# A two-layer hybrid decoder trunk on one core: element-wise work of the attention stages moved from VectorE to GpSimd, and the modulation columns from GpSimd to VectorE

## The chip, the core and the metric

The kernel runs on one core of a Trainium2 chip. A core has five engines with a queue each, and each works through its queue in order: TensorE (in the profile PE; its weight loads are shown apart as PEld), VectorE (DVE), ScalarE (ACT), GpSimd (POOL) and SyncE (SP, which issues nearly all transfers here). They wait for one another through semaphores. Matmul results lie in PSUM, everything else on the core in SBUF; GpSimd works on SBUF alone. The metric is the device time of one execution in microseconds, the median of several runs.

## The reference

Two layers over 512 tokens of width 1024. In each, six vectors (shift, scale and gate, twice) are made from a condition c; then come attention with three kinds of heads and a gated MLP.

```
for layer in range(DEPTH):                      # 2
    mod = silu(c) @ w_mod[layer] + b_mod[layer]             # 6 x 1024
    shift1, scale1, gate1, shift2, scale2, gate2 = split(mod, 6)
    h = rmsnorm(x, g_attn) * (1 + scale1) + shift1
    proj = h @ w_in
    # A: 4 heads, rotary, difference of two softmaxes (weight lam), sub-norm
    # B: 6 heads, rotary, mixture of three dilated windows
    # C: 6 heads, softmax with a cumulative forget bias
    o = concat(A, B, C)
    x = x + gate1 * (o @ w_out)
    h = rmsnorm(x, g_mlp) * (1 + scale2) + shift2
    up = h @ w_up;  u, g = up[:D_FF], up[D_FF:]             # D_FF = 2816
    x = x + gate2 * ((silu(causal_conv3(g)) * u) @ w_down)
return rmsnorm(x, g_final)
```

The rotation of A and B (`apply_rope`) is `x1*cos - x2*sin, x2*cos + x1*sin`; the kernel orders the columns so that it becomes `q*cos + swapped(q)*sin`, where the swap exchanges neighbouring rows.

## The kernel before

Activations are kept transposed: features on the 128 partitions, the 512 tokens along the free axis. Each product of a weight and an activation is made of three matmuls (`mm3`, L265 to L267): both operands are split into a rounded high part and the rest, the low part, and high x high, low x high and high x low are added up in PSUM. The high part is a copy on ScalarE into a rounding type, the low part a subtraction (`source - high`).

*Weights.* `plan` lists all weights in the order of use, tiles of 128 x 1024 for the most part. The class `Weights` loads a tile into one of three `raww` buffers (`dma`, L148, from SP's queue), makes its high part on ScalarE (`hi`, L174) and its low part on VectorE (`lo`, L186), into two buffers each (`whi`, `wlo`). `pump`, called at the steps of the chunk in progress, runs this ahead: the load two weights ahead, high and low part one ahead. A chunk (`feat_q`) is 8 steps of 3 matmuls.

*The attention of a layer* works through eight pairs of heads in the order B0 B1 A0 C0 A1 C1 B2 C2. Each pair has 8 blocks (2 heads, 4 blocks of 128 queries): scores on TensorE (`emit_S`, L631 to L641, tile `s`), masked maximum on VectorE (`emit_max`, L654, tile `e`), exponential on ScalarE (L667), transposes on TensorE (L695, tile `pt`), high and low part of the weights' transpose (L714 ScalarE, L719 VectorE), and the product with the values (L741, L742, tile `po`). In between, `fill` puts in the projections for the next pair: one chunk of queries and one of keys (`qk_chunk`, PSUM tile `qkps`) and half of a value chunk (`v_half`, `vps`), and behind the last pair the output projection (`ops`).

*A chunk's result* is worked up by `qk_post`. For A and B: ScalarE copies `qkps` to `qf` (L469); two transfers write its rows, exchanged, to `sw` (L471, L472); VectorE multiplies `qf` by the cosines (L475) and `sw` by the sines (L477) and adds them (L479). For B (and C, which has no rotation) `stack_gen` then makes high and low parts of both heads' halves, 64 rows each (L436 ScalarE, L433 VectorE), and copies them so that one matmul takes high and low rows together (L447, L449). For A, `split_gen` makes one high and one low part (L254, L256), which transfers lay out in `res`. A pair's output gets its high and low part (`oh`, `ol`) from `split_gen` too.

*Modulation.* One column of `mod` (128 features) is the sum over 1024 products of a row of `w_mod` and silu(c) (`scb`, copied to all partitions). The first 16 columns are made at the start (tile `mu`). The other 32 of layer 0 and the 48 of layer 1 are made by `mod_stream` beside other work: 24 of them (16 to 39 of layer 0) during layer 0's attention, 56 during layer 0's MLP. Each column is loaded in two halves of 256 KB into three buffers (`rawm`, L240). In the attention stage a half goes through three engines: product on GpSimd (L221), sum by an accumulating copy on ScalarE (L224), addition on VectorE (L226). In the MLP one VectorE instruction does all (L228, a product with a running sum). A last small operation makes `1 + scale` times the norm's weight (L234).

*The order.* The code is written as generators that are stepped by `tick`; a scheduler then sorts each engine's instructions by its own estimate of when they can run. So a change of engine also moves instructions that it doesn't touch.

Of the kernel before, what the change touches and what calls it, by code (L numbers as in the profile page):

```python
# [30 lines left out]
def kernel(  # L31
# [34 lines left out]
    mrp = ctx.enter_context(tc.tile_pool(name="mrp", bufs=3))  # L66
# [43 lines left out]
    lp = const.tile([128, DEPTH, 4, 32], F32, name="lp")  # L110
# [27 lines left out]
    class Weights:  # L138
# [39 lines left out]
        def lo(self, upto):  # L178
            while self.nl < min(upto, len(plan)):
# [4 lines left out]
                raw = self.raw.pop(i)  # L184
                for c, m, h, lo in self.w[i]:
                    V.tensor_tensor(out=lo[:, 0:m], in0=raw[:, c:c + m], in1=h[:, 0:m].bitcast(F32), op=ALU.subtract)  # L186
# [24 lines left out]
    def mod_col(l, ci, raws, pool=False):  # L211
        part, m = divmod(ci, 8)
        prev = bm[:, l, ci:ci + 1]
        for half in range(2):
            raw = raws(half)
            yield
            dst = modc[:, l, ci:ci + 1]
            if half == 0:
                dst = sm.tile([128, 1], F32, tag="mp", name="mp")
            if pool:  # L220
                G.tensor_tensor(out=raw, in0=raw, in1=scb[:, 512 * half:512 * half + 512], op=ALU.mult)  # L221
                yield
                d2 = sm.tile([128, 1], F32, tag="mp", name="mq")
                A.activation(out=raw, in_=raw, func=AF.Copy, accum_out=d2)  # L224
                yield
                V.tensor_tensor(out=dst, in0=d2, in1=prev, op=ALU.add)  # L226
            else:
                V.tensor_tensor_reduce(out=raw, in0=raw, in1=scb[:, 512 * half:512 * half + 512], scale=1.0, scalar=prev,  # L228
                                       op0=ALU.mult, op1=ALU.add, accum_out=dst)
            prev = dst  # L230
            yield
        if part in (1, 4):
            g = gA if part == 1 else gM
            V.scalar_tensor_tensor(out=scl[:, l, part // 4, m:m + 1], in0=modc[:, l, ci:ci + 1], scalar=1.0,  # L234
                                   in1=g[:, l, m:m + 1], op0=ALU.add, op1=ALU.mult)

    def mod_stream(l, ci):
        def raws(half):
            raw = mrp.tile([128, 512], F32, tag="raw", name="rawm")
            nc.sync.dma_start(out=raw, in_=wmod[l, ci, :, 512 * half:512 * half + 512])  # L240
            return raw
        return mod_col(l, ci, raws, l == 0 and 16 <= ci < 40)
# [10 lines left out]
    def split_gen(src, hi, lo):  # L253
        A.activation(out=hi, in_=src, func=AF.Copy)  # L254
        yield
        V.tensor_tensor(out=lo, in0=src, in1=hi.bitcast(F32), op=ALU.subtract)  # L256
# [122 lines left out]
    def layer_attn(l, ap, mods, st, rt0):  # L379
# [49 lines left out]
        def stack_gen(src, side, res, pair=None):  # L429
            R = (H0, H1)  # L430

            def sub(out, h):
                V.tensor_tensor(out=out, in0=src[R[h]], in1=res[h][R[h]].bitcast(F32), op=ALU.subtract)  # L433
# [25 lines left out]
        def qk_post(idx, side, ps, kind):  # L459
# [13 lines left out]
            for _ in range(5):  # L473
                yield
            V.tensor_tensor(out=qf, in0=qf, in1=tb[:, 0, :], op=ALU.mult)  # L475
            yield
            V.tensor_tensor(out=sw, in0=sw, in1=tb[:, 1, :], op=ALU.mult)  # L477
            yield
            V.tensor_tensor(out=qf, in0=qf, in1=sw, op=ALU.add)  # L479
# [710 lines left out]
```

## Time and profile before

| | us |
|---|---|
| median of 3 runs | 1338.51 (1336.86 to 1346.54) |
| profiled execution, its own time | 1337.11 |
| its span, first to last instruction | 1335.3 |
| layer 0: first chunk matmul of the attention (`qkps` with `whi`) | at 64.1 |
| layer 0: first matmul of the MLP (`pg`) | at 315.5 |
| layer 1: first value matmul (`vps`) | at 689.4 |
| layer 1: first matmul of the MLP (`pg`) | at 953.4 |

The granted TensorE clock is 0.989 of full speed over the span. A row of the profile's groups gives line, engine, operation, output <- inputs, shapes, how often, then busy us and mean ns of one, and at the end how long the engine stood idle just before and what ended that. A row of a timeline starts with its start and its length in us; x2 means that neighbouring instructions of one kind are merged. Lengths of matmuls are modelled: a 128x512 matmul is shown with 0.39 us, but the next one starts 0.23 us after it, as they overlap.

### The profile page before, as it was taken

Reading aid. Unit: us, or ns where it says so; the run is one execution under the profiler, and the core shown is the slowest. Engines: PE = TensorE matmul, PEld = TensorE weight load, DVE = VectorE, ACT = ScalarE, POOL = GpSimd, SP = SyncE. Lnnn points to the kernel's source line nnn. Section 1 sums busy time; section 2 is a strip of 40 time slices with the busy share of each in tenths; the row PEclk is TensorE's granted clock in tenths of the full one; section 3 lists DMA queues with packets and bytes.
Section 4 is the critical chain, followed back from the end, with each engine's and each line's share of the span. In section 5 each row is a group of like instructions: output and inputs, shape, how many; then the busy total and the mean of one; then the engine's idle time right before and its main releaser. Section 6 shows DMA issues by size and latency. Waiting matters only on the chain.

```text
span 1335.3 us, 18235 instructions
## 1 busy us (share of the span) xinstructions
PE 1278.1 (96%) x6568; PEld 1058.2 (79%) x6568; DVE 868.8 (65%) x1733; ACT 671.5 (50%) x1254; POOL 94.1 (7%) x64
## 2 busy tenths in 40 slices
PE   4899999999999999999999999999999999999997
PEld 1688787778888878888898888878878888888886
DVE  6888989868888886433347787875754444443232
ACT  5577888954433333322336677785543333333231
POOL 5232423400000000000000000000000000000000
PEclk8899999999999999999999999999999999999999
DMA  9445553432777775333333234212133333332331
GB/s 373 146 136 158 165 156 129 137 113 82 249 251 256 247 253 152 91 97 93 113 113 94 85 108 128 78 57 89 49 108 95 97 94 96 95 91 87 103 99 63
DMA packets 68127, 174.44 MB, mean 131 GB/s; under 512 B 9410, under 2 KB 11730, under 8 KB 68036
## 3 DMA queue, kind: packets, MB, share of 16 engines
q1 hardware_dynamic: 66884, 172.16, 40.9%
q8 instruction: 52, 0.85, 0.3%
q10 hardware_dynamic: 1088, 1.05, 0.2%
q14 instruction: 39, 0.32, 0.1%
q0 software_dynamic: 64, 0.06, 0.0%
HBM read 159.41 MB, written 2.10 MB: 121 GB/s over the span
## 4 chain that ended last, share of the span: by engine, by line
PE 59%; DVE 9%; DMA 6%; ACT 4%; issue 2%; SPq 0%; DVEq 0%; ACTq 0%
PE dps L265 6%; PE dps L267 6%; PE dps L266 6%; DMA rawm<-in_wmod_dram 5%; PE pg L266 4%; PE pu L265 4%; PE pg L267 4%; PE pu L267 4%; PE pu L266 4%; PE pg L265 4%; DVE wlo L186 2%; PE ops L265 2%; PE ops L266 2%; PE ops L267 2%; DVE rawm L228 2%
## 5 line engine op out<-in xcount | busy, mean ns | idle before, releaser
L186 DVE TENSOR_TENSOR wlo<-raww,whi 128x1024 fp32r<-128x1024 f32 (+3 forms) x188 | 228.2, 1214 | 232.0 <-ACT whi L174 227.8
L174 ACT ACTIVATE whi<-raww 128x1024 fp32r<-128x1024 f32 (+3 forms) x188 | 194.5, 1035 | 335.8 <-PE dps L266 137.8
L266 PE MATMUL pg<-hl,whi 128*128 128x512 f32 (+1 forms) x368 | 143.1, 389 | 0.5 <-DVE hl L314 0.2
L265 PE MATMUL pg<-hh,whi 128*128 128x512 f32 (+1 forms) x368 | 141.5, 385 | 1.6 <-ACT whi L174 1.6
L265 PE MATMUL pu<-hh,whi 128*128 128x512 f32 (+1 forms) x368 | 142.3, 387 | 0.0
L267 PE MATMUL pg<-hh,wlo 128*128 128x512 f32 (+1 forms) x368 | 141.0, 383 | 1.1 <-DVE wlo L186 1.1
L267 PE MATMUL pu<-hh,wlo 128*128 128x512 f32 (+1 forms) x368 | 140.6, 382 | 0.1
L266 PE MATMUL pu<-hl,whi 128*128 128x512 f32 (+1 forms) x368 | 140.7, 382 | 0.0
L265 PE MATMUL dps<-mh,whi 128*128 128x512 f32 x308 | 121.5, 394 | 0.0
L267 PE MATMUL dps<-mh,wlo 128*128 128x512 f32 x308 | 121.5, 394 | 0.0
L266 PE MATMUL dps<-ml,whi 128*128 128x512 f32 x308 | 121.2, 393 | 0.0
L667 ACT ACTIVATE e<-e,nm 128x256 f32<-128x256 f32 (+3 forms) x160 | 88.9, 556 | 33.9 <-DVE nm L654 30.6
L265 PE MATMUL qkps<-hh,whi 128*128 128x512 f32 x224 | 95.7, 427 | 1.0 <-ACT qf L469 0.7
L907 ACT ACTIVATE y<-y 128x512 f32<-128x512 f32 x44 | 27.8, 632 | 127.0 <-DVE y L904 117.0
L266 PE MATMUL qkps<-hl,whi 128*128 128x512 f32 x224 | 89.5, 400 | 0.0
L267 PE MATMUL qkps<-hh,wlo 128*128 128x512 f32 x224 | 89.4, 399 | 0.0
L654 DVE CUSTOM_DVE_ANT_0 e<-s,cst 128x256 f32<-128x256 f32 (+3 forms) x160 | 76.3, 481 | 17.7 <-PE s L633 6.2
L267 PEld LDWEIGHTS pg<-hh,wlo 128*128 128x128 f32 x368 | 69.0, 188 | 17.0 <-DVE wlo L186 2.4
L221 POOL TENSOR_TENSOR rawm<-rawm,scb 128x512 f32<-128x512 f32 x48 | 71.2, 1492 | 160.1 <-DMA rawm<-in_wmod_dram 115.6
L267 PEld LDWEIGHTS pu<-hh,wlo 128*128 128x128 f32 x368 | 69.1, 188 | 16.7 <-DVE wlo L186 1.2
L266 PEld LDWEIGHTS pg<-hl,whi 128*128 128x128 f32 x368 | 69.0, 188 | 16.6 <-DVE hl L314 2.0
L265 PEld LDWEIGHTS pg<-hh,whi 128*128 128x128 f32 x368 | 69.1, 188 | 16.0 <-ACT whi L174 2.0
(183 smaller groups left out, 2820.2 us busy)
## 6 DMA issues: line engine op xcount, KB each, us to landing
raww<-in_wup_dram SPq DMA_DIRECT2D x88, 512.0 KB
rawm<-in_wmod_dram SPq DMA_DIRECT2D x160, 256.0 KB
raww<-in_wqk_dram SPq DMA_DIRECT2D x32, 512.0 KB
raww<-in_wdown_dram SPq DMA_DIRECT2D x32, 512.0 KB
mu<-in_wmod_dram SPq DMA_DIRECT2D x16, 512.0 KB
raww<-in_wout_dram SPq DMA_DIRECT2D x16, 448.0 KB
raww<-in_wv_dram SPq DMA_DIRECT2D x12, 512.0 KB
raww<-in_wdown_dram SPq DMA_DIRECT2D x16, 384.0 KB
```

Source lines behind the costliest of these rows:

```text
L174: A.activation(out=h[:, 0:m], in_=self.raw[i][:, c:c + m], func=AF.Copy)
L186: V.tensor_tensor(out=lo[:, 0:m], in0=raw[:, c:c + m], in1=h[:, 0:m].bitcast(F32), op=ALU.subtract)
L221: G.tensor_tensor(out=raw, in0=raw, in1=scb[:, 512 * half:512 * half + 512], op=ALU.mult)
L228: V.tensor_tensor_reduce(out=raw, in0=raw, in1=scb[:, 512 * half:512 * half + 512], scale=1.0, scalar=prev, op0=ALU.mult, op1=ALU.add, acc ...
L265: T.matmul(ps[:, c], w[0], rhs[0][:, c], start=first, stop=False, skip_group_check=True)
L266: T.matmul(ps[:, c], w[0], rhs[1][:, c], start=False, stop=False, skip_group_check=True)
L267: T.matmul(ps[:, c], w[1], rhs[0][:, c], start=False, stop=last, skip_group_check=True)
L654: anchor[0] = V.tensor_tensor_reduce(out=e[:, 0:n], in0=s[:, 0:n], in1=cst[:, mask + SEQ - n:mask + SEQ], scale=-scale, scalar=3e38, op0=A ...
L667: anchor[1] = A.activation(out=e[:, 0:n], in_=e[:, 0:n], func=AF.Exp, bias=nm, scale=-1.0, accum_out=den).ins
L907: last_silu[0] = A.activation(out=y, in_=y, func=AF.Silu).ins
```

## The change

Of the attention stages' VectorE operations, those whose inputs both lie in SBUF go to GpSimd:

- the low parts of the weights: in each layer all of the attention's weights but the first 4 and the last 4 (25 of 33; `on_pool`);
- of the rotation, the sine product and the sum. The cosine product stays on VectorE, is now read from PSUM, and goes to a tile of its own (`qc`), the third in a pool that still has four buffers;
- the low parts of B's stacks, of A's queries and keys, and of the pairs' outputs. The low parts whose input lies in PSUM (C's stacks, L719, the values) stay.

The modulation columns all become one VectorE instruction over 1024 elements (with the running sum, both inputs in SBUF), loaded by one transfer of 512 KB into two buffers instead of three half as large. In layer 0's attention ScalarE and GpSimd have no part in them any more; the pace (`mr`) goes from 3.2 to 1.75 steps a block, as a column has 4 steps there instead of 8. The small scale operation is done once for 8 columns. The inputs of lam, `lp`, are no longer loaded at the start into a tile of their own but at block 6 into a buffer of the columns; `prep` reads them at block 10.

```diff
-    mrp = ctx.enter_context(tc.tile_pool(name="mrp", bufs=3))
+    mrp = ctx.enter_context(tc.tile_pool(name="mrp", bufs=2))
...
+        on_pool.update(range(first + 4, len(plan) - 4))
         plan += [(wup[l, j], 1024, "wp") for j in range(2 * FC)]
...
+                eng = G if i in on_pool else V
                 for c, m, h, lo in self.w[i]:
-                    V.tensor_tensor(out=lo[:, 0:m], in0=raw[:, c:c + m], in1=h[:, 0:m].bitcast(F32), op=ALU.subtract)
+                    eng.tensor_tensor(out=lo[:, 0:m], in0=raw[:, c:c + m], in1=h[:, 0:m].bitcast(F32), op=ALU.subtract)
...
+    def mod_stream(l, ci):
         part, m = divmod(ci, 8)
...
+        raw = mrp.tile([128, 1024], F32, tag="raw", name="rawm")
+        nc.sync.dma_start(out=raw, in_=wmod[l, ci])
+        yield
+        dst = modc[:, l, ci:ci + 1]
+        V.tensor_tensor_reduce(out=raw, in0=raw, in1=scb, scale=1.0, scalar=bm[:, l, ci:ci + 1],
+                               op0=ALU.mult, op1=ALU.add, accum_out=dst)
+        yield
+        yield
+        yield
+        if m < 7:
+            return
...
-    def split_gen(src, hi, lo):
+    def split_gen(src, hi, lo, eng=V):
         A.activation(out=hi, in_=src, func=AF.Copy)
         yield
-        V.tensor_tensor(out=lo, in0=src, in1=hi.bitcast(F32), op=ALU.subtract)
+        eng.tensor_tensor(out=lo, in0=src, in1=hi.bitcast(F32), op=ALU.subtract)
...
             def sub(out, h):
-                V.tensor_tensor(out=out, in0=src[R[h]], in1=res[h][R[h]].bitcast(F32), op=ALU.subtract)
+                (V if pair is not None else G).tensor_tensor(out=out, in0=src[R[h]], in1=res[h][R[h]].bitcast(F32), op=ALU.subtract)
...
-            for _ in range(5):
-                yield
-            V.tensor_tensor(out=qf, in0=qf, in1=tb[:, 0, :], op=ALU.mult)
-            yield
-            V.tensor_tensor(out=sw, in0=sw, in1=tb[:, 1, :], op=ALU.mult)
-            yield
-            V.tensor_tensor(out=qf, in0=qf, in1=sw, op=ALU.add)
+            yield
+            qc = tmp("qc", "rp")
+            V.tensor_tensor(out=qc, in0=ps, in1=tb[:, 0, :], op=ALU.mult)
+            for _ in range(4):
+                yield
+            G.tensor_tensor(out=sw, in0=sw, in1=tb[:, 1, :], op=ALU.mult)
+            yield
+            G.tensor_tensor(out=qc, in0=qc, in1=sw, op=ALU.add)
+            qf = qc
...
-                yield from split_gen(qf, hi, lo)
+                yield from split_gen(qf, hi, lo, eng=G)
...
-            yield from split_gen(op32, *res)
+            yield from split_gen(op32, *res, eng=G)
...
+            if l == 0 and b == 6:
+                lpt.append(mrp.tile([128, 1024], F32, tag="raw", name="lp")[:, 0:256].rearrange(
+                    "p (l j d) -> p l j d", l=DEPTH, j=4))
+                nc.sync.dma_start(out=lpt[0], in_=lamp)
...
-            ms, mr = 4, 3.2
+            ms, mr = 4, 1.75
```

Three places in the order of the instructions. First, VectorE where layer 1's attention begins, before (`wlo_6905` belongs to the first chunk of pair B1, `wlo_6979` to the second; `qf_6804` and `qf_6813` are B0's queries and keys, `qk` the stacked parts that the scores read):

```order
L186 TENSOR_TENSOR wlo_6905<-raww_6834,whi_6904 128x1024
L475 TENSOR_TENSOR qf_6804<-qf_6804,rope_6799 128x512
L477 TENSOR_TENSOR sw_6806<-sw_6806,rope_6799 128x512
L475 TENSOR_TENSOR qf_6813<-qf_6813,rope_6799 128x512
L477 TENSOR_TENSOR sw_6815<-sw_6815,rope_6799 128x512
L479 TENSOR_TENSOR qf_6804<-qf_6804,sw_6806 128x512
L479 TENSOR_TENSOR qf_6813<-qf_6813,sw_6815 128x512
```

The same place on GpSimd, after (`wlo_6434` and `wlo_6506` are the two weights, `qc_6361` and `qc_6363` queries and keys):

```order
L190 TENSOR_TENSOR wlo_6434<-raww_6359,whi_6433 128x1024
L469 TENSOR_TENSOR sw_6331<-sw_6331,rope_6324 128x512
L471 TENSOR_TENSOR qc_6361<-qc_6361,sw_6331 128x512
L469 TENSOR_TENSOR sw_6340<-sw_6340,rope_6324 128x512
L471 TENSOR_TENSOR qc_6363<-qc_6363,sw_6340 128x512
L424 TENSOR_TENSOR qk_6327<-qc_6361,qk_6327 64x512
L424 TENSOR_TENSOR qk_6336<-qc_6363,qk_6334 64x512
L424 TENSOR_TENSOR qk_6328<-qc_6361,qk_6328 64x512
L424 TENSOR_TENSOR qk_6337<-qc_6363,qk_6335 64x512
L190 TENSOR_TENSOR wlo_6506<-raww_6417,whi_6505 128x1024
```

Sine products, sums, low parts and weights now stand in one row on GpSimd; the second weight's low part stands behind all of them. In layer 0 the row begins with the sine product, and the first weight stands behind six of these operations.

Second, TensorE at the same place, before: the last rows ahead of the first score (tile `s`), with four more chunk matmuls ahead of these (`hh`, `hl` are the high and low part of the normed input, `qkps` the chunk's result):

```order
L266 MATMUL qkps_6967<-hl_6533,whi_6904 128x512
L267 MATMUL qkps_6967<-hh_6532,wlo_6905 128x512
L265 MATMUL qkps_6967<-hh_6635,whi_6904 128x512
L266 MATMUL qkps_6967<-hl_6636,whi_6904 128x512
L267 MATMUL qkps_6967<-hh_6635,wlo_6905 128x512
L265 MATMUL qkps_6967<-hh_6647,whi_6904 128x512
L266 MATMUL qkps_6967<-hl_6648,whi_6904 128x512
L267 MATMUL qkps_6967<-hh_6647,wlo_6905 128x512
L265 MATMUL qkps_6967<-hh_6659,whi_6904 128x512
L266 MATMUL qkps_6967<-hl_6660,whi_6904 128x512
L267 MATMUL qkps_6967<-hh_6659,wlo_6905 128x512
L631 MATMUL s_6961<-qk_6809,qk_6802 128x128
```

After, from the chunk's first matmul on:

```order
L255 MATMUL qkps_6494<-hh_6051,whi_6433 128x512
L256 MATMUL qkps_6494<-hl_6052,whi_6433 128x512
L257 MATMUL qkps_6494<-hh_6051,wlo_6434 128x512
L255 MATMUL qkps_6494<-hh_6057,whi_6433 128x512
L256 MATMUL qkps_6494<-hl_6058,whi_6433 128x512
L624 MATMUL s_6488<-qk_6334,qk_6327 128x128
L257 MATMUL qkps_6494<-hh_6057,wlo_6434 128x512
```

The first score has moved from behind 15 matmuls of the chunk to behind 5.

Third, VectorE in layer 0's attention, after, where the first columns stand (`rawm`; the row below each reads its sum out):

```order
L534 TENSOR_SCALAR z1_635<-z_371 128x24
L221 ISA rawm_735,modc_107<-rawm_735,scb_96,bm_102 128x1024
L221 ISA modc_107 128x1
L535 SCALAR_TENSOR_TENSOR z1_635<-z2_636,z1_635 128x24
L712 TENSOR_TENSOR ptl_675<-pt_737,pth_674 128x4x128
L647 ISA e_796,nm_797<-s_777,cst_94 128x384
```

A column stands as one long instruction ahead of the low part of the transpose and of the next block's maximum, where before there were two additions of one element a column.

More of the change, by code (lines that the diff above doesn't have):

```diff
@@ L109 @@
     fb = const.tile([128, DEPTH, 6], F32, name="fb")
-    lp = const.tile([128, DEPTH, 4, 32], F32, name="lp")
+    lpt = []
     modc = const.tile([128, DEPTH, 48], F32, name="modc")
@@ L113 @@
     nlam = const.tile([128, DEPTH], F32, name="nlam")
-    plan = []
+    plan, on_pool = [], set()
     for l in range(DEPTH):
+        first = len(plan)
         def qkv(idx, at="wp"):
@@ L209 @@
     W = Weights()
-    def mod_col(l, ci, raws, pool=False):
+    def mod_stream(l, ci):
         part, m = divmod(ci, 8)
-        prev = bm[:, l, ci:ci + 1]
-        for half in range(2):
-            raw = raws(half)
-            yield
[L217 to L221, printed above, removed]
-                yield
-                d2 = sm.tile([128, 1], F32, tag="mp", name="mq")
-                A.activation(out=raw, in_=raw, func=AF.Copy, accum_out=d2)
-                yield
[L226 to L231, printed above, removed]
+        raw = mrp.tile([128, 1024], F32, tag="raw", name="rawm")
[9 more added lines that the diff above has]
+            return
+        c = slice(8 * part, 8 * part + 8)
         if part in (1, 4):
             g = gA if part == 1 else gM
[L234 to L242, printed above, removed]
+            V.scalar_tensor_tensor(out=scl[:, l, part // 4, :], in0=modc[:, l, c], scalar=1.0,
+                                   in1=g[:, l, :], op0=ALU.add, op1=ALU.mult)
     def mod_gen(units, off):
@@ L366, in prep @@
     def prep():
+        lp = lpt[0]
         for l in range(DEPTH):
@@ L472, in qk_post @@
             nc.sync.dma_start(out=sw[1::2, :], in_=qf[0::2, :])
-            for _ in range(5):
+            yield
+            qc = tmp("qc", "rp")
+            V.tensor_tensor(out=qc, in0=ps, in1=tb[:, 0, :], op=ALU.mult)
+            for _ in range(4):
                 yield
-            V.tensor_tensor(out=qf, in0=qf, in1=tb[:, 0, :], op=ALU.mult)
+            G.tensor_tensor(out=sw, in0=sw, in1=tb[:, 1, :], op=ALU.mult)
             yield
-            V.tensor_tensor(out=sw, in0=sw, in1=tb[:, 1, :], op=ALU.mult)
-            yield
-            V.tensor_tensor(out=qf, in0=qf, in1=sw, op=ALU.add)
+            G.tensor_tensor(out=qc, in0=qc, in1=sw, op=ALU.add)
+            qf = qc
             yield
@@ L1061 @@
             with tc.issue_after(last_load[0]):
-                for t, a in ((fb, fbias), (cst, consts), (lp, lamp), (sg, sublng), (gM, gmlp), (gF, gfin), (cw, convw),
+                for t, a in ((fb, fbias), (cst, consts), (sg, sublng), (gM, gmlp), (gF, gfin), (cw, convw),
                              (cb, convb)):
```

## The prediction

> **What bounds the kernel now.** I read the page first (busy shares and the row of slices), then the busy time of each engine by stage, then the groups of instructions by form, and last the order of time where each layer's attention begins.
>
> ```profile
> span 1335.3 us, 18235 instructions
> PE 1278.1 (96%) x6568; PEld 1058.2 (79%) x6568; DVE 868.8 (65%) x1733; ACT 671.5 (50%) x1254; POOL 94.1 (7%) x64
> ...
> PE   4899999999999999999999999999999999999997
> DVE  6888989868888886433347787875754444443232
> POOL 5232423400000000000000000000000000000000
> ```
>
> TensorE is busy nearly everywhere, so a faster VectorE pays only where TensorE waits for it. Those places are the two attention stages. The next rows hold busy time: layer 0's attention from its first score matmul to the first gate matmul of its MLP, the same stretch of layer 1, and the MLP stretch with the modulation columns.
>
> ```profile
> core 0: us, PE busy (x) PEld busy (x) DVE busy (x) ACT busy (x) POOL busy (x), PEclk, DMA share, GB/s
> 64.80:315.50 250.70, 235.88 (x1404) 198.62 (x1403) 210.36 (x502) 195.94 (x463) 70.56 (x49) 0.99 0.44 138
> 717.70:953.40 235.70, 231.19 (x1391) 197.14 (x1391) 181.30 (x437) 165.42 (x362) 0.00 (x0) 0.99 0.30 91
> ...
> 316.00:512.00 196.00, 194.26 (x872) 157.59 (x871) 171.79 (x367) 74.68 (x101) 0.00 (x0) 1.00 0.74 236
> ```
>
> The two attention stages compute the same; layer 0 takes 250.7 - 235.7 = 15.0 us longer, at the same granted clock, and differs only in its 24 modulation columns, spread over POOL, ACT and DVE. So 15 us is what mixed-in side work costs today. Layer 1's TensorE is idle for 4.5 us only: little is to be had there.
>
> **The change, part by part.** Durations of what moves, layer 0 first, then the comparison rows of layer 1:
>
> ```profile
> L186 DVE TENSOR_TENSOR wlo<-raww,whi 128x1024 fp32r<-128x1024 f32 x21 | 28.8, 1373 | 1.3 <-ACT whi L174 1.2
> L719 DVE TENSOR_TENSOR ptl<-pt,pth 128x384 fp32r<-128x384 f32 x32 | 17.6, 550 | 3.0 <-ACT pth L714 2.7
> L433 DVE TENSOR_TENSOR qk<-qf,qk 64x512 fp32r<-64x512 f32 x11 | 10.6, 967 | 0.3
> L186 DVE TENSOR_TENSOR wlo<-raww,whi 128x896 fp32r<-128x896 f32 x7 | 8.3, 1190 | 1.7 <-ACT whi L174 1.7
> L226 DVE TENSOR_TENSOR mp<-mq,bm 128x1 f32<-128x1 f32 x24 | 8.2, 344 | 0.5 <-ACT rawm L224 0.4
> L226 DVE TENSOR_TENSOR modc<-mq,mp 128x1 f32<-128x1 f32 x24 | 7.6, 315 | 0.5 <-ACT rawm L224 0.4
> L256 DVE TENSOR_TENSOR ol<-op,oh 128x512 fp32r<-128x512 f32 x8 | 7.5, 936 | 0.7 <-ACT oh L254 0.7
> L479 DVE TENSOR_TENSOR qf<-qf,sw 128x512 f32<-128x512 f32 x8 | 5.5, 681 | 0.0
> L477 DVE TENSOR_TENSOR sw<-sw,rope 128x512 f32<-128x512 f32 x8 | 5.4, 680 | 0.0
> L256 DVE TENSOR_TENSOR qf<-qf,sw 128x512 fp32r<-128x512 f32 x4 | 3.5, 886 | 0.1
> ...
> L224 ACT ACTIVATE rawm<-rawm 128x512 f32<-128x512 f32 x48 | 29.8, 621 | 0.8 <-POOL rawm L221 0.6
> L224 ACT ACTIVATION_READ_ACCUMULATOR rawm<-rawm 128x1 f32 x48 | 9.1, 189 | 0.0
> ...
> L186 DVE TENSOR_TENSOR wlo<-raww,whi 128x1024 fp32r<-128x1024 f32 x21 | 25.6, 1218 | 7.0 <-ACT whi L174 6.9
> L719 DVE TENSOR_TENSOR ptl<-pt,pth 128x384 fp32r<-128x384 f32 x32 | 17.6, 551 | 5.1 <-ACT pth L714 5.0
> ```
>
> And what the columns cost on DVE today, and POOL's price for one product of two SBUF inputs (minimum, median, maximum ns):
>
> ```profile
> L228 DVE CUSTOM_DVE_ANT_0 rawm<-rawm,scb,mp x56: 739/751/753, 328.3 to 512.2; 128x512 f32<-128x512 f32 x56
> L221 POOL TENSOR_TENSOR rawm<-rawm,scb x48: 1264/1292/2884, 64.0 to 268.0; 128x512 f32<-128x512 f32 x48
> L1045 POOL TENSOR_TENSOR mu<-mu,scb x8: 2335/2604/3340, 9.4 to 35.9; 128x1024 f32<-128x1024 f32 x8
> ```
>
> *DVE in layer 0.* Off it go 20 low parts at 1.373 and 5 at 1.190 us (33.4), L477 and L479 (10.9), L433 from qf (10.6), L256 (11.0) and the small additions L226 (15.8): 81.7 us. The cosine product stays, read from PSUM. On it come 24 columns of 1024. No row shows that length: 0.75 us (a half's row) and 1.50 us (two halves) bound it; by the growth of L186 (1218 against 1089 ns for 128 elements more, 1.0 ns each) I estimate 0.75 + 0.51 = 1.3 us, 31 us in all. DVE falls from 210 to about 160. *ACT* loses L224, 38.9 us, and falls to 157.
>
> *POOL* gets per layer 20 parts at 2.60, 5 at 2.28 (7/8 of it) and 44 operations of 512 columns at 1.29 us (the 64-row ones counted full, as L433 costs DVE no less than L479): 52 + 11 + 57 = 120 us, half of the stage. It isn't the bound over the stage.
>
> *Do DVE and POOL hinder each other?* L186, with two SBUF inputs, takes 1373 ns beside a POOL that is 28% busy and 1218 ns beside an idle one; L719, with one input in PSUM, 550 and 551. So operations with two SBUF inputs wait for POOL's, the others don't. After the change POOL is busy half of the time, and the columns still have two SBUF inputs: scaling the 0.155 us to 48% gives 0.27 us, and to POOL's longer operations about 0.5 us a column, 12 us. DVE ends near 173 us, below layer 1's 181 today, ACT below its 165: layer 0's 15.0 us excess should go. What is late next is what layer 1 waits for now; of its 4.5 us idle I take 1.5 in each layer (ends 0 and 4.5): -3. The Trainium skill, page "SBUF — State Buffer", section "Who interferes with whom", has this as an exclusive lock: whichever of the two starts first holds the shared port for its whole instruction and the other blocks. The trace agrees with which operations clash; by the lock a column can wait for a full 2.60 us, and that is a rival below.
>
> *Where each attention begins.* Here nothing covers POOL. Layer 1, in order of time, then layer 0:
>
> ```profile
> 709.86 1.06 ACT L174 ACTIVATE whi<-raww 128x1024 fp32r<-128x1024 f32 x1 [1.58 <-PE vps L419]
> ...
> 714.50 1.28 DVE L479 TENSOR_TENSOR qf<-qf,sw 128x512 f32<-128x512 f32 x2
> 716.10 1.40 DVE L433 TENSOR_TENSOR qk<-qf,qk 64x512 fp32r<-64x512 f32 x2
> 719.04 1.23 DVE L186 TENSOR_TENSOR wlo<-raww,whi 128x1024 fp32r<-128x1024 f32 x1
> ...
> 717.01 0.63 ACT L447 ACTIVATE qk<-qf 64x512 fp32r<-64x512 f32 x1
> ...
> 717.69 0.50 PE L631 MATMUL s<-qk 128*128 128x128 f32 x2
> 719.00 0.50 PE L633 MATMUL s<-qk 128*128 128x128 f32 x2
> ...
> 719.80 0.39 PE L267 MATMUL qkps<-hh,wlo 128*128 128x512 f32 x1
> ...
> 721.19 0.39 PE L267 MATMUL qkps<-hh,wlo 128*128 128x512 f32 x1
> ...
> 57.74 0.69 DVE L475 TENSOR_TENSOR qf<-qf,rope 128x512 f32<-128x512 f32 x1 [3.83 <-DMA sw<-qf]
> ...
> 64.53 0.39 PE L267 MATMUL qkps<-hh,wlo 128*128 128x512 f32 x1
> ```
>
> POOL's row there is: one weight, two rotations (four operations), four low parts, the next weight. From 710.92 (high part done): 710.92 + 2.60 + 8 x 1.29 + 2.60 = 726.4, when the second chunk's low part is ready; today its first use is at 721.19. The first score on the way is ready at 710.92 + 2.60 + 5 x 1.29 = 720.0 instead of 717.69. TensorE's queue is in order, and the score now stands behind 5 chunk matmuls instead of 15, so nothing is left ahead of it to hide this: +5.3 us. In layer 0 the swapped copy is there at 57.74, six operations and a weight later it is 57.74 + 7.74 + 2.60 = 68.1, against 64.53: +3.6.
>
> *The other rotations* (pairs B1, A0, A1, B2 of each layer, eight): a chain of three POOL operations is 3 x (1.29 - 0.68) = 1.8 us longer, or 4.4 with a weight of 2.60 ahead of it; it may also be no longer, as DVE's queue, where L433 took 0.97 for 0.69, is emptier on POOL. Chunk and value matmuls cover most of it; I take 0.6 us each, +5 (ends 0 and 35). Two of a rotation's three tiles must come free sooner in a pool still four deep, and PSUM is held until DVE's product, at most 0.7 us longer; both are in these ends.
>
> *The last output's low part* before the closing matmuls: 1.29 for 0.68, +1.2 for both layers. *The other weights' low parts* cost nothing: W.pump makes them a chunk ahead, and a chunk is 24 matmuls of 0.23 us (six from 719.80 to 721.19), 5.5 us against 2.60; without that cover each would cost 1.4. *The MLP:* 56 columns as one operation of 1.3 for two of 0.75, from transfers of 512 KB in two buffers for 256 KB in three. TensorE is busy for 194.3 of 196.0 us and DVE has 24 us free; nothing, either way (DVE would have to wait over 0.4 us more per column to use that up).
>
> *SP's queue* issues half as many column loads, of twice the size; before, it stood still for free column buffers, with the weights' loads behind it:
>
> ```profile
> SPq L240 <- ACT rawm L224: 72.6, 37, 9.4
> ```
>
> 37 waits, 72.6 us in layer 0's attention, and TensorE didn't wait for a load there. The lam inputs now hold one of the two column buffers for four blocks, which makes such waits longer for some 2 columns: nothing, as weights are loaded two ahead; without that, about one such wait (72.6 / 37 = 2 us).
>
> Sum: -15.0 - 3.0 + 5.3 + 3.6 + 5 + 1.2 = -2.9 us. The profiled execution took 1337.11 us, so 1334.2; that execution lies 1.4 us below the median of 1338.51.
>
> **Rivals.**
> 1. *Full relief.* All idle of TensorE goes (250.7 and 235.7 both to layer 1's busy 231.2: -24.0), the rotations hide, the two beginnings stay: -24.0 + 8.9 + 1.2, 1323 us. For it: nothing but DVE and ACT makes TensorE wait. Against: POOL is slower than what it replaces at each step.
> 2. *Late chains, slower.* TensorE's and ACT's queues place scores and high parts as if POOL's results came early (as 5 for 15 above), and each of the eight rotations holds them up, with a weight's low part queued behind each sine product that waits for its transfer. At 3.5 us each: 1337.1 - 18 + 10.1 + 28 = 1357. It makes the change slower by over 1% from 2.8 us each; against it stand the chunks in between. The Trainium skill's "GPSIMD Engine Reference", section "Engine selection", advises VectorE against GpSimd for products of two inputs, at about twice the time; the trace has 1.9 (1.29 for 0.68).
> 3. *The clash eats it.* If each column waits for 2 us instead of 0.5, DVE is back at 210 and layer 0 keeps its 15 us: 1337.1 - 1.5 + 10.1 + 5 = 1351. For it: the 155 ns; against: they scale to a quarter of that. Behind a waiting column stand the next block's maximum and low part (L654, L719).
>
> **How the numbers follow.** Forecast 0.43, full relief 0.25, late chains 0.17, the clash 0.10, none of these 0.05. Within 1% (13.4 us, about what a measurement of this kernel tells from no change, 1325.1 to 1351.9): 0.39 of the forecast, 0.04 of relief, 0.03 of late chains, 0.06 of the clash, 0.52. Faster: 0.21 + 0.03 = 0.24. Slower: 0.14 + 0.04 + 0.01 + 0.05 = 0.24. The range of 1318 to 1356 reaches past relief and to late chains of 3.3 us.
>
> **What would show it.** Counted from its first chunk matmul, layer 0's attention should be some 10 us shorter (-15 - 1.5 + 3.6 + 2.5 + 0.6) and layer 1's some 7 us longer (-1.5 + 5.3 + 2.5 + 0.6); POOL near 240 us busy in the attention stages, DVE near 173 and 125. TensorE's list of waits should have scores (L624, L626 of the new kernel) behind ACT and POOL at both beginnings, 3 to 5 us each, and next to none on the weights' low parts elsewhere. I am wrong if waits on POOL's results stand at every rotation, if the columns take over 2 us each, or if the MLP's length changes.

## The result, and the profile after

| | before | after |
|---|---|---|
| median, us | 1340.67 (1336.86 to 1346.54, 4 runs) | 1407.13 (1404.02 to 1412.61, 4 runs) |
| span of the profiled execution, us | 1335.3 | 1402.7 |

The ratio is 1.050, 95% interval 1.047 to 1.053: the change made the kernel 5% slower. 1334.2 us had been forecast, from a profiled execution of 1337.1, and 1356 as the upper end.

The page of the kernel after, busy shares and some rows of slices:

```profile
span 1402.7 us, 17854 instructions
...
PE 1304.3 (93%) x6568; PEld 1078.0 (77%) x6568; DVE 789.3 (56%) x1462; ACT 641.2 (46%) x1158; POOL 258.2 (18%) x154
...
PE   4888888899999999999998989999999999999997
...
DVE  7655859565988885433353555745574444443333
...
POOL 5464242630000000000004544453000000000000
PEclk8878899999999999999999899999999999999999
```

VectorE lost 79.5 us of work and ScalarE 30.3, as intended, and yet TensorE's row falls to 8 in the slices where GpSimd works. PE has the same 6568 matmuls and is busy 26 us longer; in the same slices the granted clock falls. By stage (the two attentions, and the stretch between them; kernel after):

```profile
core 0: us, PE busy (x) PEld busy (x) DVE busy (x) ACT busy (x) POOL busy (x), PEclk, DMA share, GB/s
66.60:350.60 284.00, 252.57 (x1406) 213.90 (x1407) 186.11 (x432) 167.51 (x367) 111.67 (x64) 0.92 0.40 124
350.60:761.30 410.70, 399.35 (x1903) 328.25 (x1901) 247.93 (x364) 141.13 (x196) 8.68 (x6) 1.00 0.52 162
761.30:1021.00 259.70, 240.96 (x1402) 204.40 (x1403) 144.35 (x373) 166.15 (x363) 107.49 (x64) 0.97 0.27 82
```

Layer 0's attention took 250.7 us before and takes 284.0, layer 1's 235.7 and now 259.7. In both VectorE is busy for a smaller share than before. So no engine became the bound; something makes TensorE wait. What does, one stretch of layer 0 shows whole. The kernel after in order of time (start, length, engine, line; idle before and its cause in brackets):

```profile
88.30 2.40 POOL L190 TENSOR_TENSOR wlo<-raww,whi 128x1024 fp32r<-128x1024 f32 x1
...
89.38 1.36 DVE L533 SCALAR_TENSOR_TENSOR z<-z,z 128x24 f32<-128x24 f32 x1
...
90.66 1.26 POOL L469 TENSOR_TENSOR sw<-sw,rope 128x512 f32<-128x512 f32 x1
90.67 1.29 DVE L534 TENSOR_SCALAR z<-z 128x24 f32<-128x24 f32 x1
...
91.87 1.27 DVE L221 CUSTOM_DVE_ANT_0 rawm<-rawm,scb,bm 128x1024 f32<-128x1024 f32 x1
...
92.00 2.26 POOL L471 TENSOR_TENSOR qc<-qc,sw 128x512 f32<-128x512 f32 x1
...
93.08 1.23 DVE L535 SCALAR_TENSOR_TENSOR z<-z,z 128x24 f32<-128x24 f32 x1
...
94.23 0.68 DVE L712 TENSOR_TENSOR ptl<-pt,pth 128x512 fp32r<-128x512 f32 x1
94.30 0.63 ACT L427 ACTIVATE qk<-qc 64x512 fp32r<-64x512 f32 x1 [4.13 <-POOL qc L471]
...
94.96 0.58 PE L735 MATMUL po<-ptl,vv 128*128 128x256 f32 x1 [4.63 <-DVE ptl L712]
```

The three operations on 24 columns (z, the weights of B's windows) take 0.18 us where nothing disturbs them, and here 1.2 to 1.4. Each ends with GpSimd's instruction: L533 at 90.74, GpSimd's weight at 90.70; L534 at 91.96, the sine product at 91.92; L535 at 94.31, the sum at 94.26. It also goes the other way: the sum (L471) came 0.13 us after the column and takes 2.26 us, 1.37 being its mean. Behind the last of them in VectorE's queue stands the low part of the softmax weights (L712), for which TensorE has waited 4.63 us; ScalarE has waited 4.13 us for the sum. And then the clock (kernel after, windows before, in and behind that gap):

```profile
84.00:90.30 6.30, 6.30 (x53) 6.07 (x52) 5.79 (x12) 4.77 (x10) 5.37 (x4) 1.00 0.11 42
90.30:95.00 4.70, 0.07 (x2) 0.04 (x1) 4.70 (x7) 0.68 (x2) 3.89 (x3) 0.79 0.64 186
95.00:105.00 10.00, 10.00 (x42) 9.43 (x43) 4.17 (x15) 7.13 (x14) 5.15 (x4) 0.50 0.29 87
```

Behind the gap TensorE is granted half speed for over 10 us. So three things are at work: VectorE held, results late, and the clock lowered behind gaps.

The list of waits after (engine, line, what for; total us, times, longest):

```profile
DVE ptl L712 <- ACT pth L707: 63.4, 49, 3.7
...
ACT qk L427 <- POOL qc L471: 47.0, 12, 6.8
ACT e L660 <- DVE nm L647: 42.5, 38, 2.4
...
ACT sw L244 <- POOL qc L471: 22.6, 8, 4.2
...
PE pt L688 <- ACT e L660: 11.9, 6, 2.8
PE po L735 <- DVE ptl L712: 11.7, 11, 4.6
```

ScalarE waits 47.0 + 22.6 = 69.6 us for GpSimd's sums, at every rotation, and TensorE for what then comes late, the exponentials and the low parts.

### The profile page after: what moved, and what is told of

It reads as the page before. It is cut to its first block, busy times and chain, and to the rows that moved or that the text cites. A ratio compares the mean times of both kernels' runs of the same rounds, so it can differ in the third digit from the quotient of the medians.

```text
span 1402.7 us, 17854 instructions
## 1 busy us (share of the span) xinstructions
PE 1304.3 (93%) x6568; PEld 1078.0 (77%) x6568; DVE 789.3 (56%) x1462; ACT 641.2 (46%) x1158; POOL 258.2 (18%) x154
## 4 chain that ended last, share of the span: by engine, by line
PE 52%; DMA 8%; DVE 6%; issue 3%; ACT 3%; POOL 2%; SPq 0%; POOLq 0%; DVEq 0%; ACTq 0%
DMA rawm<-in_wmod_dram 7%; PE dps L255 6%; PE dps L257 6%; PE dps L256 6%; PE pu L255 4%; PE pu L257 4%; PE pu L256 4%; PE pg L256 4%; PE pg L257 4%; PE pg L255 4%; PE qkps L255 2%; PE qkps L256 2%; PE qkps L257 2%; DVE rawm L221 2%; DMA sw<-qf 1%
## 5 line engine op out<-in xcount | busy, mean ns | idle before, releaser
L190 DVE TENSOR_TENSOR wlo<-raww,whi 128x1024 fp32r<-128x1024 f32 (+2 forms) x138 | 164.6, 1193 | 223.2 <-ACT whi L177 219.0
L190 POOL TENSOR_TENSOR wlo<-raww,whi 128x1024 fp32r<-128x1024 f32 (+1 forms) x50 | 118.7, 2373 | 608.0 <-ACT whi L177 588.2
L221 DVE CUSTOM_DVE_ANT_0 rawm<-rawm,scb,bm 128x1024 f32<-128x1024 f32 x80 | 107.4, 1343 | 23.4 <-DMA rawm<-in_wmod_dram 23.2
L255 PE MATMUL qkps<-hh,whi 128*128 128x512 f32 x224 | 100.2, 447 | 4.8 <-DVE qc L466 2.9
L257 PE MATMUL qkps<-hh,wlo 128*128 128x512 f32 x224 | 94.3, 421 | 1.9 <-POOL wlo L190 1.9
L256 PE MATMUL qkps<-hl,whi 128*128 128x512 f32 x224 | 94.3, 421 | 0.0
L712 DVE TENSOR_TENSOR ptl<-pt,pth 128x384 fp32r<-128x384 f32 (+1 forms) x96 | 57.2, 598 | 64.2 <-ACT pth L707 63.4
L257 PEld LDWEIGHTS pu<-hh,wlo 128*128 128x128 f32 x368 | 69.1, 188 | 22.6 <-DVE wlo L190 7.5
L256 PEld LDWEIGHTS pg<-hl,whi 128*128 128x128 f32 x368 | 69.1, 188 | 17.6 <-DVE hl L304 3.1
```

The costliest lines, as they stand in the source:

```text
L190: eng.tensor_tensor(out=lo[:, 0:m], in0=raw[:, c:c + m], in1=h[:, 0:m].bitcast(F32), op=ALU.subtract)
L221: V.tensor_tensor_reduce(out=raw, in0=raw, in1=scb, scale=1.0, scalar=bm[:, l, ci:ci + 1], op0=ALU.mult, op1=ALU.add, accum_out=dst)
L255: T.matmul(ps[:, c], w[0], rhs[0][:, c], start=first, stop=False, skip_group_check=True)
L256: T.matmul(ps[:, c], w[0], rhs[1][:, c], start=False, stop=False, skip_group_check=True)
L257: T.matmul(ps[:, c], w[1], rhs[0][:, c], start=False, stop=last, skip_group_check=True)
L712: V.tensor_tensor(out=dl, in0=p3, in1=dh.bitcast(F32), op=ALU.subtract)
```

## The experiments

Called *held* below: VectorE's groups in the two attention stages, each with (its mean - its mean in e4 and e8, the two kernels without attention work on GpSimd) x its count, summed. *Longer* is what the two stages took beyond e4's 243.9 + 235.9 us (for e11, e13 and e14, which stand on e8, beyond its 244.4 + 234.6). *Half* is the time (us) in the two stages at half of the granted clock. Each ratio is to runs of the kernel before that were taken alongside.

| run | median us | ratio, 95% | longer | held | half |
|---|---|---|---|---|---|
| before | 1338.8 | | 6.6 | 14.8 | 7 |
| the change | 1407.1 | 1.047 to 1.053 | 63.9 | 33.1 | 65 |
| e1 weights and outputs only | 1383.4 | 1.028 to 1.034 | 43.4 | 36.6 | 38 |
| e2 chain only | 1376.4 | 1.023 to 1.029 | 41.4 | 11.8 | 58 |
| e3 all but the columns | 1401.8 | 1.042 to 1.049 | 67.7 | 32.3 | 75 |
| e4 columns only | 1338.0 | 0.997 to 1.000 | 0 | 0.4 | 10 |
| e5 spare reads | 1384.0 | 1.030 to 1.036 | 45.3 | 38.8 | 34 |
| e6 spare writes | 1338.5 | 0.999 to 1.001 | 2.4 | 0.2 | 10 |
| e7 steps later | 1410.1 | 1.049 to 1.056 | 65.5 | 33.0 | 71 |
| e8 columns in halves | 1331.0 | 0.992 to 0.996 | -0.8 | -0.4 | 3 |
| e9 spare reads, quarters | 1371.3 | 1.022 to 1.025 | 31.7 | 20.3 | 24 |
| e10 spare copies | 1347.0 | 1.003 to 1.006 | 11.6 | 7.2 | 20 |
| e11 spare chain | 1384.8 | 1.032 to 1.036 | 49.6 | 39.4 | 41 |
| e12 change in quarters, part of it back on VectorE | 1393.1 | 1.038 to 1.041 | 52.2 | 15.4 | 59 |
| e13 four copies late | 1358.6 | 1.012 to 1.017 | 17.9 | 3.1 | 27 |
| e14 two copies late | 1348.4 | 1.005 to 1.009 | 13.1 | 2.6 | 17 |

### e1 to e4: the change taken apart

e1 puts the rotations and the low parts of stacks and of A back on VectorE (the outputs' stay on GpSimd), e2 the weights' low parts, e3 the columns on the three engines of before, and e4 all but the columns. The outputs' low parts are on GpSimd in e1 and in e2.

```diff
# e2: the weights back
-                eng = G if i in on_pool else V
+                eng = V
# e1, likewise for each operation of the chain
-            G.tensor_tensor(out=qc, in0=qc, in1=sw, op=ALU.add)
-            qf = qc
+            V.tensor_tensor(out=qf, in0=qf, in1=sw, op=ALU.add)
...
-                yield from split_gen(qf, hi, lo, eng=G)
+                yield from split_gen(qf, hi, lo)
```

> The changed kernel with the rotation (sine product, sum, two tiles) and the low parts of B's stacks and A's queries and keys back on VectorE; the weights' and outputs' low parts stay on GpSimd, the columns on VectorE. Theory 'chain' (ScalarE's in-order queue waits for GpSimd's rotation results, TensorE starves and its clock is halved): nearly all of the loss goes, 1330 to 1350 us, ScalarE's waits for sums under 25 us (70 now), granted clock in layer 0's attention back at 0.98 or more (0.92 now). Theory 'weights' (the 50 weights' low parts on GpSimd are late or block its queue): 1380 us or more. Theory 'columns' (the 1.3 us columns hold up VectorE in layer 0): 1365 to 1385 us, with layer 0's attention still 20 us longer than layer 1's.

> The changed kernel with all weights' low parts back on VectorE; everything else as changed. Theory 'chain': GpSimd's queue loses a 2.4 us operation ahead of some rotations, but each chain of three operations stays: 1385 to 1400 us, ScalarE still waits 45 us or more for sums. Theory 'weights': 1335 to 1355 us. Theory 'columns': 1395 to 1410 us.

> The changed kernel with the modulation columns made as before (halves of 256 KB, product on GpSimd, sum on ScalarE in layer 0's attention). Theory 'chain': GpSimd gets 48 more operations of 1.3 us in layer 0, the chains there get later: 1405 to 1435 us, layer 1's attention unchanged at 260 us. Theory 'columns': layer 0's attention gets 20 us shorter, 1380 to 1390 us. Theory 'weights': 1400 to 1420 us.

> Of the whole change only the modulation columns on VectorE (one operation of 1024, two buffers, lam inputs late); all moved operations are back on VectorE. Theory 'chain': the columns alone cost little, since no GpSimd operation is beside them: 1325 to 1345 us. Theory 'columns': 1355 to 1375 us. Theory 'weights': as 'chain'.

e1 came out where 'weights' put it, e2 (1376 us) between the ranges of 'chain' and 'weights': neither part is the cause alone. The columns are neutral (e3 and e4), though in e4 one part hides another: layer 0's attention is 6.8 us shorter and the stretch behind it 6.8 longer. Either of the other parts alone lengthens the stages by 40 us or so; together they do so by less than the sum. The column *held* says more: with the weights VectorE is held for 36.6 us, about what they cost; with the chain alone for 11.8, and it costs 41.4. So the chain costs in another way too.

### e5 and e6: GpSimd works for nobody

On e4's kernel, GpSimd does something besides for each of the 25 weights of a layer, with a result that no engine waits for: in e5 the same subtraction, in e6 two writes of a constant over the same buffer.

```diff
# e5
+                    if i in on_pool:
+                        G.tensor_tensor(out=raw[:, c:c + m], in0=raw[:, c:c + m], in1=h[:, 0:m].bitcast(F32), op=ALU.subtract)
# e6
+                    if i in on_pool:
+                        G.memset(raw[:, c:c + m], 0.0)
+                        G.memset(raw[:, c:c + m], 1.0)
```

> The kernel with all attention operations back on VectorE (1338.04 us, with the columns as one operation each), and GpSimd gets in addition, for each of the 25 weights of a layer that the change had moved, a subtraction of two SBUF inputs of the same size, behind VectorE's own, whose result nobody uses. No engine waits for a result of GpSimd. Theory 'held' (VectorE's operations with two SBUF inputs are held up while GpSimd's long ones run, whatever becomes of the results): layer 0's attention lengthens by 12 to 25 us and layer 1's by 5 to 15, the column's operation rises from 1276 ns and the normalising product from 0.74 us; 1355 to 1375 us. Theory 'late' (the 33 us that the weights cost are their results coming late for TensorE and ScalarE): 1336 to 1345 us, and the two attention stages stay near 244 and 236 us.

> As the run with the spare subtractions, but GpSimd instead writes a constant twice over the same weight buffer: GpSimd is as busy with the same buffers at the same places, and reads nothing. It leaves alone what is computed. Theory 'held', if it is the reading of two inputs that holds VectorE: 1336 to 1345 us. If any work of GpSimd holds VectorE, it comes out with the spare subtractions, 1355 us or more. Theory 'late': 1336 to 1345 us as well.

e5 takes 46 us more than e4, above the expected range, and e6 nothing, though GpSimd is busy there for 90 us in the two stages and in e5 for 118. So it isn't lateness, nor the buffers, nor a busy GpSimd, but its reading. VectorE and GpSimd in order of time in e5:

```profile
83.20 2.38 POOL L192 TENSOR_TENSOR raww<-raww,whi 128x1024 f32<-128x1024 f32 x1 [5.56 <-DVE wlo L190]
83.25 2.88 DVE L426 TENSOR_TENSOR qk<-qf,qk 64x512 fp32r<-64x512 f32 x1
86.16 0.18 DVE L528 TENSOR_SCALAR z<-z 128x24 f32<-128x24 f32 x1
86.25 0.55 DVE L712 TENSOR_TENSOR ptl<-pt,pth 128x384 fp32r<-128x384 f32 x1
```

L426 comes 0.05 us after GpSimd and ends 0.55 us after GpSimd's end (85.58): it has waited for the whole instruction and then done its 0.69 us or most of it. The rows of the three kernels for this group (minimum, median and maximum ns), e5 first, then e6 and e9:

```profile
L426 DVE TENSOR_TENSOR qk<-qf,qk x11: 670/689/2881, 64.2 to 250.5; 64x512 fp32r<-64x512 f32 x11
```

```profile
L427 DVE TENSOR_TENSOR qk<-qf,qk x11: 673/687/690, 64.6 to 232.5; 64x512 fp32r<-64x512 f32 x11
```

```profile
L428 DVE TENSOR_TENSOR qk<-qf,qk x11: 673/1137/1242, 64.6 to 246.2; 64x512 fp32r<-64x512 f32 x11
```

The Trainium skill, page "SBUF — State Buffer", section "Who interferes with whom", says this: a VectorE instruction with two SBUF inputs contends with a GpSimd instruction that reads SBUF, not with one that only writes it, and the later of the two blocks until the other's end. These rows agree.

### e9 and e10: shorter instructions, fewer inputs

```diff
# e9, in place of e5's one subtraction
+                        for a in range(0, m, 256):
+                            b = min(a + 256, m)
+                            G.tensor_tensor(out=raw[:, c + a:c + b], in0=raw[:, c + a:c + b], in1=h[:, a:b].bitcast(F32), op=ALU.subtract)
# e10
+                        G.tensor_copy(out=raw[:, c:c + m], in_=h[:, 0:m].bitcast(F32))
```

> As the run with the spare subtractions of GpSimd (1383.97 us), but each in pieces of 256 columns, four instructions for one. The same bytes are read at the same places. Theory 'held whole' (an operation of VectorE with SBUF inputs that comes while GpSimd's instruction runs waits for the end of that instruction and then runs at its own speed): a wait is at most one piece, some 0.65 us in place of 2.4, the longest L426 falls from 2.9 to below 1.5 us, and the time to 1343 to 1360 us. Theory 'slowed' (both engines read at once and each goes slower): the pieces change nothing, 1376 to 1390 us.

> As the run with the spare subtractions of GpSimd (1383.97 us), but each is a copy of the high part into the weight buffer, one SBUF input for two. If only GpSimd's operations with two SBUF inputs hold VectorE: 1336 to 1342 us, with no L426 over 1 us. If every read of GpSimd does: 1355 to 1385 us. There is no reason to prefer one: the runs so far show two inputs (held) and none (not held).

In e9 the longest L428 falls from 2.88 to 1.24 us, as "held whole" has it, but the median rises: the four pieces catch more operations, each for less. *Held* falls from 38.8 to 20.3 us, and the time only to 1371, between the two ranges. Layer 1's attention has it as expected (246.3 us for e5's 257.9); layer 0's does not (265.2 for 267.2), where also a value product waits 9.1 us in three places for low parts. Why layer 0 gains so little wasn't found. e10 lies between its two ranges as well: a copy, 1.14 us long, holds VectorE also (the longest L426 is 1.52 us), for 7.2 us in all.

### e7, e13 and e14: lateness

e7 puts six more steps of other work between GpSimd's sum and ScalarE's rounding of it. e13 and e14 stand on e8's kernel and put copies in place by GpSimd behind VectorE's sum.

```diff
# e7, in the changed kernel, behind the sum
-            yield
+            for _ in range(7):
+                yield
# e13 (e14: 2)
             V.tensor_tensor(out=qf, in0=qf, in1=sw, op=ALU.add)
+            for _ in range(4):
+                G.tensor_copy(out=qf, in_=qf)
```

> The changed kernel with six more places of other work between GpSimd's sum of a rotation and ScalarE's rounding of it, so that ScalarE reaches the rounding later and finds the sum ready. Theory 'late': ScalarE's 69.6 us of waits for the sums fall below 35 us and the time to 1375 to 1395 us. Theory 'held': the waits fall as well, but VectorE's operations stay as long as they were, and the time stays within 1% of 1407 us.

> The kernel with halved columns on VectorE and nothing else of the change (1330.96 us); between VectorE's sum of each rotation and what reads it stand four copies in place by GpSimd, one SBUF input each. The sum comes some 2.4 us later (four of about 0.6), the delay that the change gave it. Copies held VectorE little (50 of 1024 columns: 7 us in all), so 80 of 512 should hold it for 6 us or less. Theory 'held and late' (of the change's 64 us in the attention stages some 25 to 30 are the rotations' results coming late for ScalarE's and TensorE's queues): 1350 to 1366 us, with waits of ScalarE for GpSimd's copies of 30 us or more. Theory 'held' alone: 1333 to 1342 us.

> As the run with four copies, but two, so that the sum comes about 1.2 us later. 'Held and late': half of the other's cost or less, 1338 to 1350 us. 'Held' alone: 1331 to 1337 us.

e7 changed nothing: ScalarE still waits 69.1 us for the sums. It decides nothing about lateness, since the wait moved with the step. e13 comes from the other side. Its copies and its waits:

```profile
L481 POOL COPY qf<-qf 128x512 f32<-128x512 f32 x80 | 65.2, 819 | 791.4 <-ACT whi L174 479.5 <-DVE qf L479 217.1 <-DMA raww<-in_wv_dram 48.0
```

```profile
ACT qk L436 <- POOL qf L481: 18.4, 9, 4.2
...
ACT sw L254 <- POOL qf L481: 10.4, 6, 2.4
```

Each sum comes 4 x 0.82 = 3.3 us later, and the kernel takes 1358.6 - 1331.0 = 27.6 us more, 1.4 a rotation, with VectorE held for 3.1 us in all. ScalarE waits 28.8 us for the copies, a little under the 30 expected. 17.9 of the 27.6 us lie in the attention stages; the first score comes 4.7 us later in layer 0, and the stretch between the attentions, with layer 1's beginning, is 4.5 longer. e14 adds 17.5 us, 63% of that for half of the delay, where half or less was expected. Lateness thus costs by itself: 4.7 and 4.5 us for the two rotations of each beginning, and at most 17.9 / 16 = 1.1 us for each of the others, the 3.1 us held included (at e10's price, 11.6 / 7.2, they would be 5 of the 17.9).

### e11 and e12: the chain, and the change in pieces

e11 has GpSimd repeat the chain behind VectorE into a tile that nobody reads; e12 was to cut each GpSimd operation of the changed kernel into pieces of 256 columns.

```diff
# e11, one of five places, on e8's kernel
             V.tensor_tensor(out=qf, in0=qf, in1=sw, op=ALU.add)
+            G.tensor_tensor(out=scrt(), in0=qf, in1=sw, op=ALU.add)
# e12, one of five places, in the changed kernel
-            G.tensor_tensor(out=qc, in0=qc, in1=sw, op=ALU.add)
+            for a in range(0, SEQ, 256):
+                G.tensor_tensor(out=qc[:, a:a + 256], in0=qc[:, a:a + 256], in1=sw[:, a:a + 256], op=ALU.add)
```

> The kernel with halved columns on VectorE and nothing else of the change (1330.96 us), and GpSimd repeats, behind VectorE, each operation of the chain that the change had moved: a rotation's sine product and sum, the stack's and A's low parts, the output's low part, 44 a layer of 512 columns, into a tile that nobody reads. Theory 'held': VectorE's operations stretch by 8 to 18 us a layer and the time is 1346 to 1368 us. Theory 'late' for this part (the chain's 24 us were its results coming late): 1329 to 1337 us.

> The changed kernel with every operation of GpSimd in the attention stages cut into pieces of 256 columns; the results are the same and come as late as before or a little later. Theory 'held whole': a wait of VectorE is at most one piece, its stretch over the kernel with the columns alone falls to a third, and of the 67 us that the change cost a third to a half goes: 1370 to 1388 us; what stays is the results coming late. If lateness is all: 1400 us or more.

e11's chain, with VectorE doing its own, holds it for 39.4 us and costs 54, more than was expected. It isn't free of waits for GpSimd: ScalarE writes A's high parts into `sw`, which the spare sums still read.

```profile
ACT sw L257 <- POOL scr L488: 23.6, 8, 5.7
```

So e11 doesn't separate holding from lateness. In the change the chain holds less (e2: 11.8): some 25 of e11's 39 us fall on VectorE's own sums and low parts of the chain, which in the change are themselves on GpSimd.

e12 does not do all that was meant: its edit of `split_gen` names VectorE, so the low parts of the outputs and of A's queries and keys, 12 in each layer, are back on VectorE in pieces. Layer 0's outputs:

```profile
L251 DVE TENSOR_TENSOR ol<-op,oh 128x256 fp32r<-128x256 f32 x16 | 7.7, 511 | 6.2 <-ACT oh L247 6.2
```

*Held* falls from 33.1 to 15.4 us (these pieces, which no other run has, are not in it) and the time by 14, less than expected. How much of that the pieces brought, and how much the move back, e12 can't say; e9 is the clean test of pieces.

### e8: the columns alone, in halves

```diff
-        return mod_col(l, ci, raws, l == 0 and 16 <= ci < 40)
+        return mod_col(l, ci, raws)
...
-            ms, mr = 4, 3.2
+            ms, mr = 4, 1.75
```

> The kernel before, with layer 0's 24 columns of modulation made by VectorE alone, in halves of 512 from three buffers of 256 KB as before (the changed kernel uses wholes of 1024 from two buffers of 512 KB). Nothing else differs, and GpSimd has no part in the attention. With the columns alone moved to wholes, layer 0's attention became 7.2 us shorter and the MLP stretch behind it 6.8 us longer. If the wholes' larger transfers lengthened the MLP, it stays at 402 us here, layer 0's attention comes to 244 to 248, and the time is 1329 to 1335 us. If it is TensorE's work itself that grows there, the time is 1336 to 1342 us.

It stands on the kernel before. By stage:

```profile
64.60:309.00 244.40, 235.52 (x1406) 199.15 (x1405) 213.12 (x550) 168.22 (x367) 0.00 (x0) 0.99 0.46 142
309.00:711.80 402.80, 399.52 (x1913) 330.69 (x1911) 261.35 (x496) 143.11 (x197) 0.26 (x1) 1.00 0.53 166
711.80:946.40 234.60, 230.30 (x1393) 195.95 (x1393) 181.51 (x437) 165.23 (x362) 0.00 (x0) 1.00 0.30 91
```

The gain in layer 0's attention stays and the MLP doesn't pay for it (402.8 us, 408.9 in e4). At 1330.96 us, ratio 0.994 (0.992 to 0.996), it is the one version here that beats the kernel before. So what e4 has in place of the halves made the MLP longer: wholes of 512 KB in two buffers, with one scale operation for 8 columns and lam's late inputs. Which of these, and by which wait, was not settled.

## Why the prediction was wrong

A gain of 2.9 us was forecast, and the kernel lost 66. The steps that failed are the price of the two engines hindering each other (12 us, and hidden in a sum), that of the late rotations (5 us), and the clock, which no step had.

*The two engines hindering each other* was seen (L186's 1373 against 1218 ns) and mis-sized. The prediction scaled 0.155 us by GpSimd's busy share, charged it to the columns alone at 0.5 us each, and added the 12 us to VectorE's sum. A mean over 21 instructions was the wrong form of it: most of them ran undisturbed, at 1.20 to 1.24 us, and five took 1.43 to 2.15. One that meets GpSimd waits for the rest of its instruction, up to 2.2 us in e5 (2.88 for 0.69). Nor were the columns the ones to pay. Their group, and one of the softmax's, layer 0's attention after:

```profile
L221 DVE CUSTOM_DVE_ANT_0 rawm<-rawm,scb,bm 128x1024 f32<-128x1024 f32 x24 | 35.7, 1487 | 0.0
...
L675 DVE SCALAR_TENSOR_TENSOR e<-e,rd 128x256 f32<-128x256 f32 x4 | 5.6, 1396 | 0.1
```

and in e4:

```profile
L221 DVE CUSTOM_DVE_ANT_0 rawm<-rawm,scb,bm 128x1024 f32<-128x1024 f32 x24 | 30.6, 1276 | 0.1
...
L673 DVE SCALAR_TENSOR_TENSOR e<-e,rd 128x256 f32<-128x256 f32 x4 | 1.9, 482 | 0.0
```

The columns pay 5.1 of the 23.2 us that VectorE is held there; the rest falls on z, A's normalising products and other small operations, which no step of the prediction counted. The length of a column, 1.3 us by the estimate, was right (1276 ns in e4).

*The reckoning by sums* failed with it. The prediction set VectorE's total (173 us) against layer 1's (181) and let layer 0's 15 us of excess go. After, VectorE has 186 and 144 us in stages of 284 and 260. It is idle for over a third of the time and TensorE still waits, since each block's softmax passes through VectorE's queue in order, and a hold of 1 to 2 us can delay the whole step. Where spare work on GpSimd reads two inputs and nothing waits for it (e5, e9) the stages grew by 1.2 to 1.6 us for each us held. By that, as an estimate, 33.1 us held makes 40 to 53 of the change's 63.9. The price isn't fixed: the kernel before has 14.8 us held, and its stages are only 6.6 us longer than e4's.

*The 15 us of excess* were mis-sized too: with the columns on VectorE alone, layer 0's attention is 6.3 (e8) or 6.8 us (e4) shorter.

*The other rotations*, 0.6 us for each of eight pairs with ends 0 and 35 us for all: in e13, with sums 3.3 us late, the stages grew by 17.9 us, up to 2.2 for each pair (two chunks), and in the change the low parts, late too, come on top. The mechanism was rightly named and priced at about a quarter. "Next to none on the sums elsewhere" was not what the waits showed: ScalarE stood at every rotation, as the prediction had said would prove it wrong.

*The beginnings*, +5.3 and +3.6, were right, and a little small. After, first layer 0, then layer 1:

```profile
68.69 0.50 PE L257 MATMUL qkps<-hh,wlo 128*128 128x512 f32 x1 [1.21 <-POOL wlo L190]
...
751.15 1.06 ACT L177 ACTIVATE whi<-raww 128x1024 fp32r<-128x1024 f32 x1 [1.58 <-PE vps L410]
...
761.33 0.31 PE L624 MATMUL s<-qk 128*128 128x128 f32 x1 [4.58 <-POOL qk L424]
...
770.02 0.50 PE L257 MATMUL qkps<-hh,wlo 128*128 128x512 f32 x1 [0.73 <-POOL wlo L190]
```

In layer 0 the first low part is used at 68.69 (forecast 68.1, before 64.53): +4.2. In layer 1, counted from the high part's end at 752.21, the first score comes after 9.1 us (forecast 9.1, before 6.8) and the second chunk's low part is used after 17.8 (forecast 15.5, before 10.3): +7.5. The first score of layer 0 came only 1.3 us later than in e4 (66.6 against 65.3).

*The other weights' low parts cost nothing*: right for lateness, as TensorE waits 1.9 us in all for GpSimd's `wlo`; wrong in what it left out, since they held VectorE, which e1 and e5 price at some 45 us. *The MLP, nothing:* the columns as changed cost 6.8 us there (e4).

*The clock* was in no term. At equal numbers of matmuls TensorE is busy for 252.6 + 241.0 us in the two stages, in e4 for 236.0 + 231.6: 25.9 of the 63.9 us are slower matmuls, 38.0 are idle. They come behind idle time: each of the change's eleven stretches at half clock in the two stages begins behind 3.4 us in which TensorE was idle for 1.5 to 2.7 us. That this is the only cause isn't shown: two of e4's three stretches have less than 0.3 us idle there.

Of the rivals, "late chains" and "the clash" were both true at once, the second larger than priced and elsewhere. How the rest of the chain's cost in e2 (41.4 us with 11.8 held) divides between late sums, late low parts and the clock stays open.

## What to carry to other kernels

Before moving work to GpSimd, list which VectorE operations read SBUF alone, those with two inputs first, and what waits behind them in its queue: one that meets a GpSimd instruction that reads SBUF waits for its end, and if a softmax or another chain from engine to engine stands behind, the stage can grow by more than what was held (1.2 to 1.6 us for each us in e5, e9 and e10, under 0.5 in the kernel before), though VectorE is idle for part of it. A spare copy of the work on GpSimd, whose result nobody reads, prices that apart from lateness in one run, if no engine writes what the copy still reads. What GpSimd can do for nothing here is to write.

## What the runs showed of the hardware

- A GpSimd subtraction of 128x1024 held VectorE instructions of 0.18 to 0.7 us until its end; one input read (a copy of 1.14 us) also held, but less (7.2 us for 50 copies, 38.8 for 50 subtractions); writes alone (two of 0.95 us each) held nothing.
- An operation of one SBUF input was held too: L534, a TENSOR_SCALAR of 128x24, took 1.29 us, and TENSOR_SCALAR rows in e4 take 0.17 to 0.18. The low part from PSUM (L712, 128x384) took 551 ns after and 552 in e4.
- Cutting GpSimd's instruction into quarters halved what was held and added to its own time: 886 ns for 256 columns, 2483 for 1024.
- One gap of 4.7 us in a stage where TensorE is over 85% busy (from 90.3) saw the clock fall to half within it, at 93.0, for 13.7 us. All such stretches in the stages were 3.4, 6.8, 10.2 or 13.7 us long; the Trainium skill, page "TensorE: Matmul & The Clock Gate", section "What's actually happening", gives a window of 3413 ns by which the clock is decided, and these lengths agree.
